# Attention scores: the product with the low parts of the keys on 128 rows, the low keys padded by rows of zeros

## The chip, the cores and the metric

The kernel runs on one core of a Trainium2 chip. The metric is the device time of one execution in microseconds (us); lower is better. The time before is the median of three runs.

## What is computed

The reference applies two layers to 1024 tokens of width 2048. A layer normalises the tokens, multiplies them by a wide input matrix, runs three mixers side by side (sliding-window attention, a gated spatial mixer, gated linear attention), gates their outputs, multiplies them by an output matrix and adds the result to the input. Only the scores of the attention matter here:

```python
scores = jnp.einsum('bnqgrd,bnkgd->bngrqk', qb, kb) * (SWA_HEAD_DIM ** -0.5)
```

There are 16 query heads of 64 dimensions in 4 groups; a group of 4 query heads shares one key head. The 1024 tokens are cut into blocks of 128 queries, and a block sees 256 keys: its own block and the one before it.

## The kernel before, in words

Each layer is worked in two halves of 512 tokens, so there are four phases, each an input part and an output part. Nearly all of TensorE's work is in the projections, `mm_f` (lines 390 to 392) and `mm_t` (lines 382 to 384). An fp32 value is split there into a high part in fp32r and a low part that holds the rest; a product is made of three matmuls (high by high, high by low, low by high). The weights come by DMA into `wraw`, ScalarE rounds them to their high part (line 368), VectorE subtracts to get the low part (line 369), and the pair stands in `whl`, of which there are three buffers.

The mixers run between these projections. They are generators in lanes (`att`, `gla`, `sg`, `mod`); `tick` is called after each k-tile of a projection's output tile and steps the lanes that are due. So the order in which the work is written down is fixed by counts of projection matmuls; the framework then orders each engine's instructions by priority when the program is built, and each engine runs its list in that order.

In an attention step, `att_split` has made `qs`, a tile with two heads p = 0 and 1. For each of them it holds the high part of the query on 64 of the 128 rows, and its low part on the other 64. `split_keys` has made, for each key head g, `kh[g]`, which holds the high part of the key on both halves of the rows, so that one matmul on 128 rows gives high by high plus low by high. The low parts of two key heads share one tile `kl[j]`: that of head 2j on rows 0 to 63, that of head 2j + 1 on rows 64 to 127. The third product, the query's high part by the key's low part, therefore runs on 64 rows. The scores of a block go into a PSUM tile `mx` that is shared by two blocks (b = 0, 1), one such tile for each p; PSUM has two `mx` buffers for all the mixers. The first block of the sequence has no block before it, so its matmuls take 128 columns and not 256. After the scores, ScalarE and VectorE copy them out of PSUM (lines 503 to 506).

In a phase there are 8 attention steps of 2 block pairs, each with 2 blocks and 2 heads, so 64 products with `kh` and 64 with `kl`. VectorE also carries the last 128 keys of the first half over to the second half (lines 459 and 463).

Of the kernel before, what the change touches and what calls it, by code (L numbers as in the profile page):

```python
# [10 lines left out]
F32 = mybir.dt.float32  # L11
F32R = mybir.dt.float32r
# [4 lines left out]
ALU = mybir.AluOpType  # L17
# [4 lines left out]
P = 128  # L22
# [4 lines left out]
H = SEQ // NH  # L27
# [13 lines left out]
def hybrid_kernel(ctx: ExitStack, tc: tile.TileContext, a, y_out):  # L41
# [11 lines left out]
    pools = {}  # L53

    V, S, G, PE = nc.vector, nc.scalar, nc.gpsimd, nc.tensor

    def load(out, in_):
        nc.sync.dma_start(out=out, in_=in_)
# [9 lines left out]
    def start(name, gen):  # L68
        lanes.setdefault(name, [deque(), None, 0])[0].append(gen)
# [36 lines left out]
    def mxt():  # L106
        return mx.tile([P, 512], F32, tag="mx", name="mx")
# [4 lines left out]
    def col(n, name):  # L112
        return sm.tile([P, n], F32, tag=name, name=name)
# [301 lines left out]
    def att():  # L415
        return pools["at"].tile([P, 512], F32, tag="at", name="at")

    def rope(dst, raw, cst):
        sh = att()
        V.stream_shuffle(sh, raw, swap)  # L420
        V.tensor_tensor(dst, raw, cst[0], ALU.mult)
        V.tensor_tensor(sh, sh, cst[1], ALU.mult)
        V.tensor_tensor(dst, dst, sh, ALU.add)
# [29 lines left out]
    def split_keys(j, kr, first):  # L453

        for p in range(2):
            g = 2 * j + p
            r, o = slice(64 * p, 64 * p + 64), slice(64 - 64 * p, 128 - 64 * p)
            if not first:
                V.tensor_copy(kh[g][:, 0:P], kh[g][:, H:H + P].bitcast(F32))
            S.copy(kh[g][r, P:], kr[r])  # L460
            S.copy(kh[g][o, P:], kr[r])
        if not first:
            V.tensor_copy(kl[j][:, 0:P], kl[j][:, H:H + P].bitcast(F32))
        for p in range(2):
            r = slice(64 * p, 64 * p + 64)
            V.tensor_tensor(kl[j][r, P:], kr[r], kh[2 * j + p][r, P:].bitcast(F32), ALU.subtract)

    def att_split(q):

        qs = pools["qs"].tile([P, 2, H], F32R, tag="qs", name="qs")  # L470
        for p in range(2):
            r, o = slice(64 * p, 64 * p + 64), slice(64 - 64 * p, 128 - 64 * p)
            S.copy(qs[r, p], q[r])
            V.tensor_tensor(qs[o, p], q[r], qs[r, p].bitcast(F32), ALU.subtract)
        return qs

    def attention(l, h, g0, qt, vt, cst):

        rope(qt[0], qt[0], cst)
        yield 5  # L480
        qs = att_split(qt[0])
        yield 6
        for m in range(4):
            i = 4 * g0 + m
            j = i // 4
            M = pools["m"].tile([P, 2, NT, P], F32, tag="M", name="M")
            for bp in range(2):
                sps = [mxt().rearrange("p (b k) -> p b k", b=2) for _ in range(2)]
                for b in range(2):
                    n = 2 * bp + b  # L490
                    k0 = P if h == 0 and n == 0 else 0
                    for p in range(2):
                        PE.matmul(sps[p][:, b, k0:], lhsT=qs[:, p, n * P:(n + 1) * P],  # L493
                                  rhs=kh[2 * j + p][:, n * P + k0:n * P + 256], start=True, stop=False)
                    for p in range(2):
                        rows = slice(64 * p, 64 * p + 64)
                        PE.matmul(sps[p][:, b, k0:], lhsT=qs[rows, p, n * P:(n + 1) * P],  # L497
                                  rhs=kl[j][rows, n * P + k0:n * P + 256], start=False, stop=True)
                for p in range(2):
                    sp = sps[p]  # L500
                    if h == 0 and bp == 0:
                        G.memset(M[:, p, 0], -1e30)
                        S.copy(M[:, p, 1], sp[:, 1, 0:P])
                    else:
                        S.copy(M[:, p, 2 * bp:2 * bp + 2], sp[:, :, 0:P])  # L505
                    V.copy_predicated(M[:, p, 2 * bp:2 * bp + 2], pmask.unsqueeze(1).broadcast_to([P, 2, P]),  # L506
                                      sp[:, :, P:2 * P])
                yield LAG["s"][bp]
            Mf = M.rearrange("p a b k -> p (a b) k")
            mxv = col(8, "at_mx")  # L510
            V.tensor_reduce(mxv, Mf, AX.X, ALU.max)
            nm = col(8, "at_nm")
            ns = nsink[l][:, 2 * i:2 * i + 2].unsqueeze(2).broadcast_to([P, 2, NT])
            V.scalar_tensor_tensor(nm.rearrange("p (a b) -> p a b", a=2), mxv.rearrange("p (a b) -> p a b", a=2),  # L514
                                   -0.125, ns, ALU.mult, ALU.min)
            es = col(8, "at_es")
            V.tensor_tensor(es.rearrange("p (a b) -> p a b", a=2), nm.rearrange("p (a b) -> p a b", a=2), ns,
                            ALU.subtract)
            S.activation(es, es, AF.Exp)
            den = col(8, "at_den")  # L520
            for k in range(8):
                S.activation(Mf[:, k], Mf[:, k], AF.Exp, bias=nm[:, k:k + 1], scale=0.125, accum_out=den[:, k:k + 1])  # L522
            V.tensor_tensor(den, den, es, ALU.add)
            V.reciprocal(den, den)
            V.tensor_tensor(Mf, Mf, den.unsqueeze(2).broadcast_to([P, 8, P]), ALU.mult)
            if m < 3:
                yield 4
                rope(qt[m + 1], qt[m + 1], cst)
                yield 5
                qs = att_split(qt[m + 1])  # L530
                yield LAG["e"] - 9
            else:
                yield LAG["e"]
            pts = []
            for p in range(2):
                tp = mxt()
                for n in range(NT):
                    PE.transpose(tp[:, n * P:(n + 1) * P], M[:, p, n], ident)  # L538
                pt = pools["pt"].tile([P, 2, NT, P], F32, tag="PT", name="PT")
                V.tensor_tensor(pt, tp.rearrange("p (n q) -> p n q", n=NT).unsqueeze(1).broadcast_to([P, 2, NT, P]),  # L540
                                amask.unsqueeze(2).broadcast_to([P, 2, NT, P]), ALU.mult)
                pts.append(pt)
                yield LAG["t"][p]
            yp = mxt()
            for n in range(NT):
                prev = not (h == 0 and n == 0)
                for w in range(2 if prev else 1):
                    for p in range(2):
                        g = 2 * j + p
                        vv = vt[n + 1 - w]  # L550
                        PE.matmul(yp[64 * p:64 * p + 64, n * P:(n + 1) * P], lhsT=vv[:, g * 64:g * 64 + 64],  # L551
                                  rhs=pts[p][:, w, n], start=(w == 0), stop=(w == 1 or not prev))
            yt = att()
            S.activation(yt, yp, AF.Copy, scale=0.5)
            load(y_d[h][i], yt)
            yield 2
# [198 lines left out]
    def in_phase(l, h, slots, pre=None):  # L755
# [18 lines left out]
        def keys(kraw):  # L774
            for j in range(2):
                rope(kraw[j], kraw[j], cst)
                yield 5
                split_keys(j, kraw[j], h == 0)
                yield 5
# [23 lines left out]

        qt = evac(4, io_tile, proj_f(512, slots))
        start("att", attention(l, h, 0, qt, vt, cst))
        cv = evac(4, hold, proj_t(512, slots))
        start("gla", gla_b(cv))
        ps = proj_f(512, slots)
        drain("att", until=lambda: lanes["att"][1] is None)
        qt = evac(4, io_tile, ps)  # L810
        start("att", attention(l, h, 1, qt, vt, cst))

        ps = proj_t(512, slots)
# [198 lines left out]
    with tc.tile_pool(name="start", bufs=1) as st:  # L1012
# [92 lines left out]
        for c in range(8):  # L1105
            for q in range(8):
                mod_load(8 * c + q + WM0 - 1)
                w = ws.popleft()
                for kk in range(2):
                    k = 2 * q + kk  # L1110
                    r = 32 * (k % 4)
# [40 lines left out]
                       ("ma", 1), ("kk", 1)):  # L1152
        pools[name] = ctx.enter_context(tc.tile_pool(name=name, bufs=bufs))
    kh = [pools["kk"].tile([P, P + H], F32R, name=f"kh{g}") for g in range(4)]
    kl = [pools["kk"].tile([P, P + H], F32R, name=f"kl{j}") for j in range(2)]
    start("mod", iter((60,)))
    for n in range(4):
        start("mod", mod_chunk(0, 8 + n))
# [115 lines left out]
```

## Time and profile before

| what | value |
|---|---|
| median of 3 runs | 3167.28 us (3166.84 to 3167.59) |
| the profiled execution | 3170.71 us, its span 3169.0 us |
| TensorE matmuls (PE) | 3095.0 us busy, 98% of the span, 17346 matmuls |
| TensorE weight loads (PEld) | 2459.1 us, 78% |
| VectorE (DVE) | 1838.1 us, 58% |
| ScalarE (ACT) | 1207.0 us, 38% |
| GpSimd (POOL) | 41.3 us, 1% |
| mean granted clock of TensorE | 0.990 of full speed |

The profiled execution took 3170.71 us, of which 3169.0 us lie between the first and the last instruction. A busy share says how long at least one instruction of the engine was in flight. Matmuls follow each other in a pipeline, so one is in flight longer than the distance from its start to the next one's start; it is this distance that a long row of matmuls costs.

### The profile page before, as it was taken

To read this page: it belongs to the slowest core of one execution; us is meant where nothing else is said; L and a number is where in the kernel's file an instruction comes from. 1 tells how busy PE (TensorE), PEld (TensorE's weight loads), DVE (VectorE), ACT (ScalarE), POOL (GpSimd) and SP (SyncE) were. 2 spreads that over 40 slices of the span, in tenths; PEclk is the share of its full clock that TensorE was granted. 3 is DMA by queue.
4 is the path that set the end of the run, shared out by engine and by line. 5 is a ranking of instruction groups with operands and counts; after the bars stand their busy time and mean duration, and the time that the engine had idled before them with its cause. 6 is when DMAs were issued, how large, how long until landed. Compare 5 with 4: busy or idle time off the path is not lost.

```text
span 3169.0 us, 44364 instructions
## 1 busy us (share of the span) xinstructions
PE 3095.0 (98%) x17346; PEld 2459.1 (78%) x17346; DVE 1838.1 (58%) x2953; ACT 1207.0 (38%) x2399; POOL 41.3 (1%) x80
## 2 busy tenths in 40 slices
PE   6999999999999999999999999999999999999998
PEld 2477777888878777888888877788888877788886
DVE  3268777665676877745355676644346475653425
ACT  3144437332344444323234454432223544432323
POOL 2000000000000000000000000000000000000000
PEclk8999999999999999999999999999999999999999
DMA  9754446566676335544346322334446322333535
GB/s 330 231 162 135 134 129 194 184 194 205 199 232 193 118 115 164 181 142 149 120 120 188 94 75 89 111 112 135 121 125 203 97 83 84 103 120 111 165 103 167
DMA packets 224195, 468.99 MB, mean 148 GB/s; under 512 B 21584, under 2 KB 77296, under 8 KB 223984
## 3 DMA queue, kind: packets, MB, share of 16 engines
q1 hardware_dynamic: 223984, 466.15, 47.8%
q8 instruction: 136, 2.23, 0.3%
q14 instruction: 75, 0.61, 0.1%
HBM read 429.37 MB, written 36.70 MB: 147 GB/s over the span
## 4 chain that ended last, share of the span: by engine, by line
PE 82%; DVE 7%; DMA 7%; ACT 2%; issue 2%; SPq 0%; DVEq 0%; ACTq 0%
PE pj L382 13%; PE pj L383 12%; PE pj L384 12%; PE pj L390 12%; PE pj L392 11%; PE pj L391 11%; DMA wm<-in_w_mod_dram 4%; PE mx L551 2%; PE mx L497 2%; PE mx L493 1%; PE pj L1112 1%; DVE ma L225 1%; DVE whl L369 1%; DMA t<-in_gla_norm_g_dram 1%; PE mx L538 1%
## 5 line engine op out<-in xcount | busy, mean ns | idle before, releaser
L369 DVE TENSOR_TENSOR whl<-wraw,whl 128x1024 fp32r<-128x1024 f32 (+3 forms) x512 | 590.9, 1154 | 740.7 <-ACT whl L368 739.0
L368 ACT CAST whl<-wraw 128x1024 fp32r<-128x1024 f32 (+3 forms) x512 | 509.0, 994 | 1108.3 <-PE pj L392 508.5
L390 PE MATMUL pj<-whl,act 128*128 128x512 f32 (+1 forms) x2048 | 792.2, 387 | 1.4 <-ACT whl L368 1.0
L392 PE MATMUL pj<-whl,act 128*128 128x512 f32 (+1 forms) x2048 | 779.7, 381 | 0.0
L391 PE MATMUL pj<-whl,act 128*128 128x512 f32 (+1 forms) x2048 | 777.5, 380 | 1.1 <-DVE whl L369 1.1
L382 PE MATMUL pj<-act,whl 128*128 128x512 f32 x1904 | 753.8, 398 | 3.6 <-ACT whl L368 1.9
L384 PE MATMUL pj<-act,whl 128*128 128x512 f32 x1904 | 745.6, 392 | 1.3 <-DVE whl L369 1.2
L383 PE MATMUL pj<-act,whl 128*128 128x512 f32 x1904 | 744.8, 391 | 0.3 <-DVE act L279 0.3
L390 PEld LDWEIGHTS pj<-whl,act 128*128 128x128 f32 x2048 | 386.1, 189 | 79.6 <-issue 6.0
L392 PEld LDWEIGHTS pj<-whl,act 128*128 128x128 f32 x2048 | 386.1, 189 | 73.9 <-issue 0.7
L391 PEld LDWEIGHTS pj<-whl,act 128*128 128x128 f32 x2048 | 386.6, 189 | 69.7 <-DVE whl L369 1.7
L382 PEld LDWEIGHTS pj<-act,whl 128*128 128x128 f32 x1904 | 357.5, 188 | 103.9 <-issue 20.4
L384 PEld LDWEIGHTS pj<-act,whl 128*128 128x128 f32 x1904 | 358.0, 188 | 85.5 <-issue 7.3
L383 PEld LDWEIGHTS pj<-act,whl 128*128 128x128 f32 x1904 | 358.4, 188 | 77.4 <-issue 5.9
L225 DVE SCALAR_TENSOR_TENSOR ma<-wm,sc,ma 128x512 f32<-128x512 f32 x240 | 179.8, 749 | 107.6 <-DMA wm<-in_w_mod_dram 105.2
L522 ACT ACTIVATE M<-M,at_nm 128x128 f32<-128x128 f32 x256 | 99.4, 390 | 47.6 <-DVE at_nm L514 45.1
L506 DVE COPY_PREDICATED M<-pmask,mx 128x256 f32<-128x256 uint8 x128 | 51.6, 443 | 91.4 <-ACT M L505 79.0
L540 DVE TENSOR_TENSOR PT<-mx,amask 128x1024 f32<-128x1024 f32 x64 | 78.0, 1220 | 24.3 <-PE mx L538 24.2
L1112 PE MATMUL pj<-wm,scb 128*32 128x512 f32 x256 | 66.8, 666 | 24.5 <-DMA wm<-in_w_mod_dram 24.5
L505 ACT COPY M<-mx 128x256 f32<-128x256 f32 x96 | 32.0, 375 | 133.0 <-PE mx L497 132.9
L551 PE MATMUL mx<-PT,v 128*64 128x128 f32 x960 | 67.9, 287 | 12.1 <-DVE PT L540 12.1
L551 PEld LDWEIGHTS mx<-PT,v 128*64 128x64 f32 x960 | 57.2, 143 | 26.7 <-DVE PT L540 14.8
(229 smaller groups left out, 2391.4 us busy)
## 6 DMA issues: line engine op xcount, KB each, us to landing
wraw<-in_w_in_dram SPq DMA_DIRECT2D x312, 512.0 KB, 3.6
wraw<-in_w_out_dram SPq DMA_DIRECT2D x136, 512.0 KB, 3.6
wm<-in_w_mod_dram SPq DMA_DIRECT2D x256, 256.0 KB, 3.3
wm<-in_w_mod_dram SPq DMA_DIRECT2D x64, 512.0 KB, 6.2
y<-at SPq DMA_DIRECT2D x64, 256.0 KB, 2.6
q<-y SPq DMA_DIRECT2D x64, 256.0 KB, 3.3
q<-x SPq DMA_DIRECT2D x36, 256.0 KB, 2.8
wraw<-in_w_vcg_dram SPq DMA_DIRECT2D x32, 272.0 KB, 2.8
```

The costliest lines, as they stand in the source:

```text
L225: V.scalar_tensor_tensor(acc, ws[k], sc[:, k:k + 1], acc, ALU.mult, ALU.add)
L368: S.copy(hl[:, 0], raw)
L369: V.tensor_tensor(hl[:, 1], raw, hl[:, 0].bitcast(F32), ALU.subtract)
L382: PE.matmul(ps, lhsT=whi, rhs=slot[:, 0], start=(k == 0), stop=False)
L383: PE.matmul(ps, lhsT=whi, rhs=slot[:, 1], start=False, stop=False)
L384: PE.matmul(ps, lhsT=wlo, rhs=slot[:, 0], start=False, stop=(k == NK - 1))
L390: PE.matmul(ps, lhsT=slot[:, 0, c], rhs=whi, start=(k == 0), stop=False)
L391: PE.matmul(ps, lhsT=slot[:, 0, c], rhs=wlo, start=False, stop=False)
L392: PE.matmul(ps, lhsT=slot[:, 1, c], rhs=whi, start=False, stop=(k == NK - 1))
L522: S.activation(Mf[:, k], Mf[:, k], AF.Exp, bias=nm[:, k:k + 1], scale=0.125, accum_out=den[:, k:k + 1])
L551: PE.matmul(yp[64 * p:64 * p + 64, n * P:(n + 1) * P], lhsT=vv[:, g * 64:g * 64 + 64], rhs=pts[p][:, w, n], start=(w == 0), stop=(w == 1 o ...
L1112: PE.matmul(mps[r:r + 32, :], lhsT=scb[:, k], rhs=w[:, kk], start=(k < 4), stop=(k >= 12))
```

## The change

The low keys get a tile for each key head, `kl[0]` to `kl[3]`, of 128 rows. The head's low keys stand on the same 64 rows as before; the other 64 rows are set to zero once, at the start, by GpSimd. The third product of the scores then takes all 128 rows of `qs` and of `kl`: the query's low part, which is on the other 64 rows, meets zeros. The order in the source also changes, from both heads' `kh` products followed by both heads' `kl` products, to `kh` and `kl` of one head followed by those of the other. In `split_keys` the copy of the last 128 keys is made for each head on 64 rows, and not for both heads together on 128 rows.

```diff
             S.copy(kh[g][r, P:], kr[r])
             S.copy(kh[g][o, P:], kr[r])
-        if not first:
-            V.tensor_copy(kl[j][:, 0:P], kl[j][:, H:H + P].bitcast(F32))
-        for p in range(2):
-            r = slice(64 * p, 64 * p + 64)
-            V.tensor_tensor(kl[j][r, P:], kr[r], kh[2 * j + p][r, P:].bitcast(F32), ALU.subtract)
+            if not first:
+                V.tensor_copy(kl[g][r, 0:P], kl[g][r, H:H + P].bitcast(F32))
+            V.tensor_tensor(kl[g][r, P:], kr[r], kh[g][r, P:].bitcast(F32), ALU.subtract)
...
                     for p in range(2):
-                        PE.matmul(sps[p][:, b, k0:], lhsT=qs[:, p, n * P:(n + 1) * P],
-                                  rhs=kh[2 * j + p][:, n * P + k0:n * P + 256], start=True, stop=False)
-                    for p in range(2):
-                        rows = slice(64 * p, 64 * p + 64)
-                        PE.matmul(sps[p][:, b, k0:], lhsT=qs[rows, p, n * P:(n + 1) * P],
-                                  rhs=kl[j][rows, n * P + k0:n * P + 256], start=False, stop=True)
+                        for part, keys in enumerate((kh, kl)):
+                            PE.matmul(sps[p][:, b, k0:], lhsT=qs[:, p, n * P:(n + 1) * P],
+                                      rhs=keys[2 * j + p][:, n * P + k0:n * P + 256], start=(part == 0), stop=(part == 1))
...
-    kl = [pools["kk"].tile([P, P + H], F32R, name=f"kl{j}") for j in range(2)]
+
+    kl = [pools["kk"].tile([P, P + H], F32R, name=f"kl{g}") for g in range(4)]
+    for g in range(4):
+        G.memset(kl[g][64 - 64 * (g % 2):P - 64 * (g % 2)].bitcast(F32), 0.0)
```

## Rows read from the trace of the kernel before

**Rows 1.** The page's busy time: share of the span and count by engine.

```profile
PE 3095.0 (98%) x17346; PEld 2459.1 (78%) x17346; DVE 1838.1 (58%) x2953; ACT 1207.0 (38%) x2399; POOL 41.3 (1%) x80
```

**Rows 2.** The page's chain that ended last, by engine.

```profile
PE 82%; DVE 7%; DMA 7%; ACT 2%; issue 2%; SPq 0%; DVEq 0%; ACTq 0%
```

**Rows 3.** Engines' busy us (count), sum of 270:512, 1048:1290, 1790:2040, 2540:2790, each with attention.

```profile
sum 984.00, PE 964.34 PEld 756.09 DVE 678.07 ACT 431.45 POOL 4.95; mean PE 241.09 PEld 189.02 DVE 169.52 ACT 107.86 POOL 1.24
```

**Rows 4.** Waits of ScalarE and of TensorE: us in total, times, longest.

```profile
ACT whl L368 <- PE pj L392: 508.5, 156, 6.2
...
PE mx L551 <- DVE PT L540: 12.1, 5, 4.2
```

**Rows 5.** Groups of score matmuls by line: durations in ns, minimum, median, maximum.

```profile
L493 PE MATMUL mx<-kh,qs x256: 218/282/580, 271.8 to 2784.8; 128*128 128x256 f32 x105, 128*128 128x128 f32 x23
...
L497 PE MATMUL mx<-kl,qs x256: 322/381/579, 272.1 to 2785.0; 64*128 64x256 f32 x106, 64*128 64x128 f32 x22
```

**Rows 6.** Timeline of TensorE, both heads together: start, us, engine, line, operation.

```profile
2783.94 0.40 PE L493 MATMUL mx<-kh,qs 128*128 128x256 f32 x2
2784.27 0.38 PE L497 MATMUL mx<-kl,qs 64*128 64x256 f32 x2
2784.58 0.50 PE L493 MATMUL mx<-kh,qs 128*128 128x256 f32 x2
2785.01 0.39 PE L497 MATMUL mx<-kl,qs 64*128 64x256 f32 x2
2785.33 0.50 PE L390 MATMUL pj<-whl,act 128*128 128x512 f32 x1
2785.67 0.40 PE L391 MATMUL pj<-whl,act 128*128 128x512 f32 x1
2785.90 0.39 PE L392 MATMUL pj<-whl,act 128*128 128x512 f32 x1
```

**Rows 7.** Timeline of TensorE, one head alone.

```profile
1052.12 0.28 PE L493 MATMUL mx<-kh,qs 128*128 128x256 f32 x1
1052.33 0.38 PE L497 MATMUL mx<-kl,qs 64*128 64x256 f32 x1
1052.63 0.38 PE L493 MATMUL mx<-kh,qs 128*128 128x256 f32 x1
1052.95 0.38 PE L497 MATMUL mx<-kl,qs 64*128 64x256 f32 x1
1053.26 0.50 PE L392 MATMUL pj<-whl,act 128*128 128x512 f32 x1
1053.60 0.40 PE L390 MATMUL pj<-whl,act 128*128 128x512 f32 x1
```

**Rows 8.** Timeline of TensorE: first `kl` product alone, first pair, last one alone.

```profile
272.06 0.32 PE L497 MATMUL mx<-kl,qs 64*128 64x128 f32 x1
...
277.23 0.53 PE L497 MATMUL mx<-kl,qs 64*128 64x256 f32 x2
...
2754.75 0.38 PE L497 MATMUL mx<-kl,qs 64*128 64x256 f32 x1
```

**Rows 9.** Timeline of TensorE, a row of matmuls of 272 columns: first and twelfth.

```profile
205.15 0.29 PE L391 MATMUL pj<-whl,act 128*128 128x272 f32 x1
...
206.53 0.29 PE L390 MATMUL pj<-whl,act 128*128 128x272 f32 x1
```

**Rows 10.** Timeline of the weight loads, at the stretch of rows 9 and of rows 6.

```profile
205.15 0.19 PEld L392 LDWEIGHTS pj<-whl,act 128*128 128x128 f32 x1
...
2785.33 0.19 PEld L390 LDWEIGHTS pj<-whl,act 128*128 128x128 f32 x1
```

**Rows 11.** VectorE's copy and subtraction for `kl`, and a memset of GpSimd.

```profile
L466 DVE TENSOR_TENSOR kl<-t,kh x16: 676/686/692, 180.6 to 2464.1; 64x512 fp32r<-64x512 f32 x16
L463 DVE CAST kl<-kl x4: 210/217/223, 185.0 to 1717.7; 128x128 fp32r<-128x128 f32 x4
...
L601 POOL MEMSET hold<- 128x512 f32 x16 | 8.4, 527 | 1351.6 <-DMA x<-hold 647.1 <-DMA out_dram<-hold 329.8 <-DVE el L684 191.5
```

## The prediction

> **What bounds the kernel now.** I read four views in this order: the page's busy times, the chain of waits that ended last, the waits engine by engine, and then the timeline of TensorE where the change acts. The busy times show matmuls in flight for 98% of the span while VectorE has 58% and ScalarE 38% [rows 1]. That alone would not prove a bound, since a matmul in flight may be a waiting one. The chain shows the same from the other end: 82% of the span is TensorE's own work, VectorE and DMA come in with 7% each [rows 2]. The waits settle it. ScalarE, which starts the split of the weights, has waited 508.5 us for line 392 alone, that is, for a projection to give a weight buffer back, while TensorE's waits for the attention's transposed probabilities come to 12.1 us in the whole run [rows 4]. The helpers wait for TensorE and not the other way round. So a microsecond that TensorE saves in these stretches should come off the time nearly whole, as long as the others keep up.
>
> How much of TensorE's time can the scores be? The two lines have 256 matmuls each [rows 5]. Their durations don't tell, since matmuls overlap; the starts do. In the long row of 272-column matmuls on 128 rows, eleven steps take 206.53 − 205.15 = 1.38 us, 0.125 us each [rows 9], and a 512-column matmul is followed by the next after 2785.90 − 2785.67 = 0.23 us [rows 6]. The line through the two points gives about 0.12 us for 256 columns. Eight score products of a block pair would take 0.96 us at that pace. The timeline shows 1.50 us: from the first `kh` at 2783.94 to the second projection matmul after the scores at 2785.67 it is 1.73 us, of which 0.23 us belong to the first projection matmul [rows 6]. I count up to that second matmul because the first one, in flight for 0.50 us and followed after 0.34 us rather than 0.23, carries a part of the delay.
>
> Where the time goes can be read in the same lines. The two `kl` products, on rows 0 to 63 and 64 to 127, run side by side: both together are in flight for 0.39 us [rows 6], which is what one takes, 381 ns [rows 5]. But the next 128-row matmul starts only 0.31 to 0.32 us after them. The weight load shows why: in the steady row a load of 0.19 us begins while the matmul before is running, at 205.15 for the matmul that comes one step later; after a 64-row product the load begins at 2785.33, together with its own matmul [rows 10]. Each passage from 128 rows to 64 and back thus empties TensorE's pipeline.
>
> The passages don't always serve two heads. In other block pairs only one head's PSUM buffer was free when the order was made, and TensorE goes `kh`, `kl`, `kh`, `kl` for that head, some projection matmuls, and the same for the other head. Four products then take 1053.60 − 1052.12 − 0.23 = 1.25 us [rows 7], against 0.48 at the steady pace. Walking the timeline through all four phases I count 91 visits to 64 rows by a pair of `kl` products and 74 by one alone (2 × 91 + 74 = 256); the first and the last of each kind: pairs 277.23 [rows 8] to 2785.01 [rows 6], alone 272.06 to 2754.75 [rows 8].
>
> **The change part by part.** *The products.* After the change all 512 are 128-row matmuls like their neighbours, at 0.12 us.
> - A pair visit saves (1.50 − 0.96) / 2 = 0.27 us; 91 of them 24.6 us. The loss of the side-by-side run is in this figure: three product times become four.
> - A visit alone saves (1.25 − 0.48) / 2 = 0.385 us; 74 of them 28.5 us.
> - Together 53 us.
>
> The 64 products of 128 columns (32 on each line; the first block of the sequence) are in this as if they were 256 wide. By the line through the two paces they could take 0.06 us, which would add at most 64 × 0.06 = 4 us to the gain; the bounds of this term are 53 and 57.
>
> At this place a rule of the skill speaks for the change and another against it. The page TensorEngine Tiling (Array Packing) of the Trainium skill, Tiling Modes, says that changing the tiling mode drains TensorE; the delays behind the `kl` products agree with it, and by it the sum stands as above. The page TensorE: Matmul & The Clock Gate of the Trainium skill, Why this matters for your kernels, advises the opposite: a product of few rows takes as long as one of 128, and the gain of row slices is that several run at the same time, so this change would only lose. The pairs do run at the same time here, but by that rule alone the time would rise by 11 us; it is the first rival below.
>
> *The order of the source.* `kl` now follows `kh` of the same head, into the same PSUM columns. The 272-column row does just that, three products in turn into one tile, at 0.125 us [rows 9], so I give it no cost. If the order on TensorE still goes by heads when only one buffer is free, it costs nothing either, since there is no passage left.
>
> *VectorE and ScalarE.* The 16 subtractions stay as they are, 64 rows of 512. The 4 copies of 128 rows become 8 of 64; a copy took 217 ns [rows 11], and if 64 rows take as long, VectorE does 4 × 0.22 = 0.9 us more in the whole run. It is hidden: the subtractions begin at 180.6 [rows 11] and the first product that reads them at 272.1 [rows 5], 91 us later. Without that cover it would be those 0.9 us. The new order of the lines in `split_keys` may move a subtraction by one ScalarE copy; the same 91 us cover it.
>
> *GpSimd.* Four memsets of 64 rows by 640 columns. The nearest row has 512 columns on 128 rows at 527 ns [rows 11], so some 0.66 us each, 2.6 us on an engine that is busy for 1% [rows 1]. They come before the first subtraction and once only. At worst VectorE stands for these 2.6 us near 180 us with weight splits queued behind it; I count nothing, and keep 2.6 us for the range.
>
> *What comes late next.* In the four stretches with attention matmuls are in flight for 964.34 of 984.00 us, so 19.7 us are idle, and VectorE is busy for 678.07 us, 69% [rows 3]. Without 53 us the stretches last 931 us and VectorE's share is 73%. The stretches' idle time is bounded below by growing not at all; above, I let it double, 20 us. VectorE's load rises only by a twentieth, and the split's waits say that the buffers come from TensorE [rows 4], so I take a value near the lower end, 4 us.
>
> *Sum.* 53 − 4 = 49 us off the profiled execution's 3170.71 us gives 3121.7. That execution lies 3.4 us above the median of the three runs, 3167.28; against the median the same sum gives **3118 us**. Of the profiled time 1.7 us lie outside the span of 3169.0 and are untouched.
>
> **The rivals.**
> 1. *The delay does not come from the number of rows* (slower). It might come with short matmuls whose weights are new, or with the return to a PSUM tile just written, and stay. Then only the side-by-side run is lost: 91 × 0.12 = 11 us more, 3178 us. The price of the delay now is 0.39 us for a pair visit (0.27 + 0.12) and 0.385 for one alone, 64 us in all, so slower is decided when less than a sixth of it (11 of 64) goes. For it: two things change at each passage, the line and the rows. Against it: the 272-column matmuls are almost as short, have new weights each, write the same tile three times in a row and show no delay [rows 9]. Chance 0.04.
> 2. *Weight loads become the limit.* A load takes 0.19 us [rows 10]. If in the short products it could not run under the matmul before, a product would cost at least 0.19 rather than 0.12: 512 × 0.07 = 36 us of the 53 gone, 3150 us with no further loss. Against it stand the loads of 0.19 us that begin every 0.125 us [rows 9, 10]. Chance 0.04.
> 3. *The gain is had on TensorE and partly given back*: VectorE, a DMA or another order of the instructions around the scores takes half of it, 27 us; 3140 us. For it: VectorE has 69% in these stretches [rows 3], and attention steps are placed by counts of projection matmuls, which now go by faster. Against it: ScalarE's long waits for buffers [rows 4]. Chance 0.13.
> 4. *All of it is given back*, because the stretches are in truth set by a chain through VectorE: 3167 us. The idle time of only 19.7 us in 984 [rows 3] leaves little room. Chance 0.03.
>
> **How the numbers follow.** My forecast as told has the remaining chance, 0.76, and by itself a range of 3110 (57 us gained and no new wait, against the median) to 3130 (the 53 us less 13 us of waits and the memsets' 3). I let the range reach 4 us further down, for the paces that I read to 0.01 us (0.01 us on 512 products is 5 us), so it goes from 3106 to 3142, which takes in rival 3 as well; rivals 1, 2 and 4, 0.11 together, lie outside. A measurement of this kernel can tell about 0.2%, 6 us, from no change. Faster: the forecast, rival 2 and rival 3, 0.93, less 0.01 for the far end of rival 2 (at 0.22 us for a product the whole gain would be gone, 512 × 0.10 = 51 us): 0.92. Same: rival 4 and that 0.01: 0.04. Slower: rival 1, 0.04.
>
> **What would show it.** In the profile after, the score lines should have only 128-row forms; a block pair's eight products should take about 0.96 us from the first start to the second projection matmul, less 0.23, where it is 1.50 now; the weight load behind the last of them should begin before its own matmul. TensorE's idle time in the attention stretches should grow by no more than some microseconds, and each of the four stretches be shorter by about a quarter of the whole gain. The parts without attention should last as long as before. The prediction is wrong if starts 0.2 us or more apart remain between the score products (rivals 1 and 2), or if they are gone and the gaps stand elsewhere, at the probabilities' transposes or the weight splits (rivals 3 and 4).

## The result and the profile after

The changed kernel takes 0.9853 of the time before (95% interval 0.9839 to 0.9868), 1.5% less, or 46.6 us of 3167.44. Its four runs have a median of 3126.42 us (3122.08 to 3129.4). The two medians are 41.0 us apart, a little less than the interval gives (41.8 to 51.0 us), so the gain is known to within some 5 us. The profiled execution took 3122.08 us, 48.6 us less than the one profiled before; it was the fastest of its four. The forecast was 3118 us in a range of 3106 to 3142.

The page of the kernel after, its busy times and its chain by engine, answers to [rows 1, 2]:

```profile
span 3120.4 us, 44382 instructions
...
PE 3042.7 (98%) x17346; PEld 2448.0 (78%) x17346; DVE 1837.3 (59%) x2957; ACT 1206.2 (39%) x2399; POOL 43.4 (1%) x84
...
PE 82%; DVE 8%; DMA 5%; ACT 2%; issue 2%; SPq 0%; DVEq 0%; ACTq 0%
```

The count of matmuls is the same, 17346, and TensorE is still what bounds the kernel: 98% of the span and 82% of the chain. VectorE has four instructions more (the copies by head), GpSimd four (the memsets).

The timeline of TensorE after the change, for the block pair that stands in [rows 6]:

```profile
2735.33 0.40 PE L392 MATMUL pj<-whl,act 128*128 128x512 f32 x1
2735.56 0.28 PE L492 MATMUL mx<-kh,qs 128*128 128x256 f32 x1
2735.68 0.28 PE L492 MATMUL mx<-kl,qs 128*128 128x256 f32 x1
2735.80 0.28 PE L492 MATMUL mx<-kh,qs 128*128 128x256 f32 x1
2735.92 0.28 PE L492 MATMUL mx<-kl,qs 128*128 128x256 f32 x1
2736.04 0.28 PE L492 MATMUL mx<-kh,qs 128*128 128x256 f32 x1
2736.16 0.28 PE L492 MATMUL mx<-kl,qs 128*128 128x256 f32 x1
2736.28 0.28 PE L492 MATMUL mx<-kh,qs 128*128 128x256 f32 x1
2736.40 0.28 PE L492 MATMUL mx<-kl,qs 128*128 128x256 f32 x1
2736.52 0.39 PE L390 MATMUL pj<-whl,act 128*128 128x512 f32 x1
2736.75 0.40 PE L391 MATMUL pj<-whl,act 128*128 128x512 f32 x1
```

Every product starts 0.12 us after the one before it, and the projection matmul behind them is followed after 0.23 us as anywhere else. From the first start to the second projection matmul it is 1.19 us; less 0.23 that leaves 0.96, where [rows 6] gave 1.50. The weight loads of the same stretch answer to [rows 10]:

```profile
2736.28 0.19 PEld L492 LDWEIGHTS mx<-kl,qs 128*128 128x128 f32 x1
2736.40 0.19 PEld L390 LDWEIGHTS pj<-whl,act 128*128 128x128 f32 x1
2736.52 0.19 PEld L391 LDWEIGHTS pj<-whl,act 128*128 128x128 f32 x1
```

The load for L390's matmul, which starts at 2736.52, begins at 2736.40, together with the last `kl` product. Before, a load behind a `kl` product began with its own matmul.

Where did the 48.6 us come from? The windows below are cut in each kernel from its first to its last score product in a phase. First come the four windows of the kernel before and their sum, then those of the kernel after (columns: window; us; busy us and count of PE, PEld, DVE, ACT and POOL; granted clock of TensorE; busy share of the DMA engines; GB/s):

```profile
271.80:508.10 236.30, 227.13 (x1491) 176.64 (x1491) 173.22 (x296) 101.57 (x281) 2.47 (x14) 0.97 0.46 141
1050.40:1282.30 231.90, 227.77 (x1536) 177.88 (x1535) 171.17 (x292) 100.70 (x265) 0.00 (x0) 0.98 0.44 137
1812.30:2032.80 220.50, 218.06 (x1487) 171.40 (x1487) 141.36 (x246) 98.65 (x265) 2.48 (x14) 1.00 0.30 90
2560.90:2784.80 223.90, 221.66 (x1523) 174.45 (x1523) 140.12 (x242) 100.51 (x265) 0.00 (x0) 0.99 0.30 89
sum 912.60, PE 894.63 PEld 700.38 DVE 625.88 ACT 401.43 POOL 4.95; mean PE 223.66 PEld 175.09 DVE 156.47 ACT 100.36 POOL 1.24
```

```profile
270.50:493.80 223.30, 213.32 (x1492) 172.81 (x1493) 172.72 (x296) 101.14 (x281) 2.46 (x14) 0.98 0.48 148
1033.60:1253.10 219.50, 212.76 (x1535) 174.17 (x1536) 170.27 (x292) 100.35 (x265) 0.00 (x0) 0.99 0.47 144
1782.70:1995.10 212.40, 208.35 (x1489) 170.20 (x1488) 141.22 (x246) 98.65 (x265) 2.48 (x14) 0.99 0.31 93
2522.80:2736.30 213.50, 210.08 (x1525) 172.50 (x1525) 139.87 (x242) 100.09 (x265) 0.00 (x0) 0.99 0.31 92
sum 868.70, PE 844.51 PEld 689.68 DVE 624.09 ACT 400.22 POOL 4.94; mean PE 211.13 PEld 172.42 DVE 156.02 ACT 100.06 POOL 1.24
```

The four stretches are 43.9 us shorter. Matmuls are in flight for 50.1 us less, and TensorE's idle time in them grew from 18.0 to 24.2 us (912.60 − 894.63, 868.70 − 844.51), 6.2 us. VectorE does the same work as before, in less time: its share went from 69% to 72%. The granted clock of the four stretches was 0.97, 0.98, 1.00 and 0.99 before and 0.98, 0.99, 0.99 and 0.99 after; by an estimate from these figures (length times the missing share) some 3 us of the 43.9 go with the clock and not with the products, and why it differs is not shown. The other 4.7 us lie outside these stretches. TensorE is idle there for 2.9 us less than before, all of it ahead of the second stretch; executions of one kernel differ by more (fifteen of the kernel before lie between 3166.36 and 3176.27 us), so this is not shown to be the change's doing.

### The profile page after: what moved, and what is told of

Read it like the earlier page. It is cut to its first block, busy times and chain, and to the rows that moved or that the text cites. A ratio compares the mean times of both kernels' runs of the same rounds, so it can differ in the third digit from the quotient of the medians.

```text
span 3120.4 us, 44382 instructions
## 1 busy us (share of the span) xinstructions
PE 3042.7 (98%) x17346; PEld 2448.0 (78%) x17346; DVE 1837.3 (59%) x2957; ACT 1206.2 (39%) x2399; POOL 43.4 (1%) x84
## 4 chain that ended last, share of the span: by engine, by line
PE 82%; DVE 8%; DMA 5%; ACT 2%; issue 2%; SPq 0%; DVEq 0%; ACTq 0%
PE pj L382 13%; PE pj L383 12%; PE pj L384 12%; PE pj L390 12%; PE pj L392 12%; PE pj L391 12%; DMA wm<-in_w_mod_dram 2%; PE mx L546 2%; PE mx L492 2%; PE pj L1107 1%; DVE whl L369 1%; DMA t<-in_gla_norm_g_dram 1%; DVE ma L225 1%; DMA t<-in_x_dram 1%; PE mx L533 1%
## 5 line engine op out<-in xcount | busy, mean ns | idle before, releaser
L390 PE MATMUL pj<-whl,act 128*128 128x512 f32 (+1 forms) x2048 | 785.5, 384 | 1.0 <-ACT whl L368 1.0
L390 PEld LDWEIGHTS pj<-whl,act 128*128 128x128 f32 x2048 | 385.3, 188 | 72.7 <-issue 5.6
L1107 PE MATMUL pj<-wm,scb 128*32 128x512 f32 x256 | 67.0, 665 | 24.2 <-DMA wm<-in_w_mod_dram 24.2
L501 DVE COPY_PREDICATED M<-pmask,mx 128x256 f32<-128x256 uint8 x128 | 51.6, 442 | 57.3 <-ACT M L500 48.5
```

Of the source, the lines that this page charges most:

```text
L390: PE.matmul(ps, lhsT=slot[:, 0, c], rhs=whi, start=(k == 0), stop=False)
L1107: PE.matmul(mps[r:r + 32, :], lhsT=scb[:, k], rhs=w[:, kk], start=(k < 4), stop=(k >= 12))
```

## The experiments

Three theories were put to the test. **V**: each visit of TensorE to 64 rows costs about 0.39 us beyond its products, the change takes all 165 visits away, and that is the whole gain, less 0.12 us for each pair that no longer runs side by side. **O**: the gain comes from the new order, `kl` right behind `kh` of the same head, with the same weights and the same PSUM tile. **S**: it comes from the separate `kl` tiles and the waits that go with them.

**e1, the padded rows in the old order.** The edit is shown against the kernel after.

```diff
-                    for p in range(2):
-                        for part, keys in enumerate((kh, kl)):
+                    for part, keys in enumerate((kh, kl)):
+                        for p in range(2):
                             PE.matmul(sps[p][:, b, k0:], lhsT=qs[:, p, n * P:(n + 1) * P],
```

> The low keys padded by zeros and all products on 128 rows, but in the order of the source before: both heads' kh, then both heads' kl. Theory V (each visit of TensorE to 64 rows costs about 0.39 us; the change takes all 165 visits away): as the changed kernel, 3126 us, within 10 us; a block pair's eight products 0.96 us. Theory O (the gain comes from the order, kl right behind kh of the same head, with the same weights and the same PSUM tile): most of the gain is lost, 3155 to 3178 us.

Measured: 0.9859 of the time before (0.9846 to 0.9873), median 3125.79 us. Each of the two ratios, this one and the changed kernel's 0.9853, lies in the other's interval. With 128 rows the order is worth nothing that can be measured, which speaks against O.

**e2, the new order on 64 rows.** The edit is shown against the kernel before.

```diff
                     for p in range(2):
                         PE.matmul(sps[p][:, b, k0:], lhsT=qs[:, p, n * P:(n + 1) * P],
                                   rhs=kh[2 * j + p][:, n * P + k0:n * P + 256], start=True, stop=False)
-                    for p in range(2):
                         rows = slice(64 * p, 64 * p + 64)
                         PE.matmul(sps[p][:, b, k0:], lhsT=qs[rows, p, n * P:(n + 1) * P],
```

> kl stays on 64 rows in the two shared tiles; only the order of the source is that of the change, kh and kl of one head, then of the other. In the program's order TensorE goes to 64 rows 254 times, where the kernel before does 165 times. Theory V: 89 visits more at 0.39 us, and about 89 fewer side-by-side runs at 0.12 us: 35 + 11 = 46 us slower than before, 3213 us. Theory O: as the changed kernel, about 3126 us.

Measured: 1.0136 (1.0122 to 1.015), which is 43 us more than before, where V gave 46. The median is 3213.11 us; that it meets V's 3213 to the microsecond is chance, since the kernel before had a median of 3171.14 us beside it. The timeline of one block pair in this kernel:

```profile
2829.84 0.28 PE L493 MATMUL mx<-kh,qs 128*128 128x256 f32 x1
2830.05 0.38 PE L496 MATMUL mx<-kl,qs 64*128 64x256 f32 x1
2830.36 0.38 PE L493 MATMUL mx<-kh,qs 128*128 128x256 f32 x1
2830.67 0.38 PE L496 MATMUL mx<-kl,qs 64*128 64x256 f32 x1
2830.98 0.38 PE L493 MATMUL mx<-kh,qs 128*128 128x256 f32 x1
2831.30 0.38 PE L496 MATMUL mx<-kl,qs 64*128 64x256 f32 x1
2831.61 0.38 PE L493 MATMUL mx<-kh,qs 128*128 128x256 f32 x1
2831.92 0.38 PE L496 MATMUL mx<-kl,qs 64*128 64x256 f32 x1
2832.23 0.50 PE L390 MATMUL pj<-whl,act 128*128 128x512 f32 x1
2832.57 0.40 PE L391 MATMUL pj<-whl,act 128*128 128x512 f32 x1
```

Four visits instead of two: 2832.57 − 2829.84 − 0.23 = 2.50 us, and (2.50 − 0.96) / 4 = 0.385 us for each visit, the price that [rows 7] gave. The order is that of the change line for line, and the weights come from the same `qs`; what differs from the timeline of the kernel after is the rows (and the shared `kl` tile, which e4 shows to cost nothing). O is refuted.

**e3, 64 rows, but half as many visits.** The second block of a pair does `kl` before `kh`, so that the `kl` products of both blocks follow each other. The edit is against the kernel before; the lines that it takes out are left out here.

```diff
...
+                    for part in ("hi", "lo") if b == 0 else ("lo", "hi"):
+                        first = (part == "hi") == (b == 0)
                         for p in range(2):
...
+                            PE.matmul(sps[p][:, b, k0:], lhsT=qs[rows, p, n * P:(n + 1) * P],
+                                      rhs=keys[rows, n * P + k0:n * P + 256], start=first, stop=not first)
```

> kl stays on 64 rows in the two shared tiles; in the second block of a pair kl goes ahead of kh, so that the kl products of both blocks follow each other. In the program's order TensorE goes to 64 rows 87 times (before: 165). Theory V: 78 visits fewer at 0.39 us: 30 us faster than before, 3137 us. If the delay belonged to each kl product or to the change of tile and not to the visit, it would stay at 3167 us.

Measured: 0.9913 (0.9898 to 0.9928), median 3144.78 us, 27 to 28 us less than before by the ratio, where V gave 30. The same products on the same rows cost less when they are visited together:

```profile
410.15 0.40 PE L392 MATMUL pj<-whl,act 128*128 128x512 f32 x1
410.39 0.40 PE L499 MATMUL mx<-kh,qs 128*128 128x256 f32 x2
410.71 0.50 PE L499 MATMUL mx<-kl,qs 64*128 64x256 f32 x4
411.15 0.51 PE L499 MATMUL mx<-kh,qs 128*128 128x256 f32 x2
411.49 0.40 PE L390 MATMUL pj<-whl,act 128*128 128x512 f32 x1
411.73 0.40 PE L391 MATMUL pj<-whl,act 128*128 128x512 f32 x1
```

One visit: 411.73 − 410.39 − 0.23 = 1.11 us. Four `kh` at 0.12, two pairs side by side at 0.12 and one visit at 0.39 make 0.48 + 0.24 + 0.39 = 1.11.

**e4, all of the change but its products.** The products are those of before, on 64 rows; each reads its head's own tile. The line shown is the one in which the products differ from those of the kernel before.

```diff
-                                  rhs=kl[j][rows, n * P + k0:n * P + 256], start=False, stop=True)
+                                  rhs=kl[2 * j + p][rows, n * P + k0:n * P + 256], start=False, stop=True)
```

> All of the change but its products: four kl tiles with zero rows, the memsets, the copies by head; the products read 64 rows in the old order. 165 visits as before. Theory V: as before, 3167 us, within 6 us. Theory S (the separate tiles, and waits of VectorE that go with them, bring the gain): about 3126 us.

Measured: 1.0005 (0.9997 to 1.0014). The tiles, memsets and copies cost and bring nothing that can be told from no change. S is refuted.

**e5, no zeros.** The rows that the change pads hold the low keys too. The edit is against the kernel after.

```diff
-                V.tensor_copy(kl[g][r, 0:P], kl[g][r, H:H + P].bitcast(F32))
+                V.tensor_copy(kl[g][:, 0:P], kl[g][:, H:H + P].bitcast(F32))
             V.tensor_tensor(kl[g][r, P:], kr[r], kh[g][r, P:].bitcast(F32), ALU.subtract)
+            V.tensor_tensor(kl[g][o, P:], kr[r], kh[g][r, P:].bitcast(F32), ALU.subtract)
...
-    for g in range(4):
-        G.memset(kl[g][64 - 64 * (g % 2):P - 64 * (g % 2)].bitcast(F32), 0.0)
```

> The changed kernel without the zeros and the memsets: the other 64 rows of each kl tile hold the low keys as well, so the low query by low key product is added (a fourth term that the other kernels leave out), at the price of 16 more subtractions on VectorE, 0.69 us each, 11 us in all. Theory V: the matmuls don't care what stands in the rows; as the changed kernel, 3126 us, within 6 us. If the zeros themselves helped (a higher granted clock, or less work), it would be slower than that, towards 3167 us, at a lower clock.

Measured: 0.9868 (0.9851 to 0.9884), median 3129.85 us, granted clock 0.992 against 0.991. The interval holds the changed kernel's 0.9853. What stands in the other rows makes no difference that can be told, and the 16 subtractions more are hidden.

**e6 and e7, the length of a visit.** Both make each `kl` product five times, e6 on 64 rows in the order of e3, e7 on 128 rows in the order of the change. This is the main line of e7's edit, against the kernel after; e6 makes the same repetition in e3's loop.

```diff
-                        for part, keys in enumerate((kh, kl)):
+                        for part, keys in enumerate((kh, kl, kl, kl, kl, kl)):
...
```

> The kernel with fewer visits, each kl product made five times on 64 rows (the low part of the scores is five times too large; its time alone counts): 1024 products more, about as many visits (85). Theory V with the two heads side by side for most of them: some 870 at 0.06 us and the rest at 0.12 us: 70 us more than the kernel with fewer visits, about 3215 us. Without a gain from running side by side: 1024 x 0.12 = 123 us more, 3268 us.

> The changed kernel with each kl product made five times on 128 rows (the low part of the scores five times too large, as in the run beside it): 1024 products more at 0.12 us, 123 us: 3249 us. Theory V: here the kernel on 64 rows should be the faster of the two, since a visit costs 0.39 us and a pair side by side saves 0.12 us, so that a visit pays from about three and a quarter pairs on. If 128 rows are better whatever the length of a visit, this one stays 20 us or more below the other.

Measured: e6 1.0212 (1.0196 to 1.0229), median 3238.8 us; e7 1.0269 (1.0254 to 1.0284), 3257.92 us. With long visits the 64 rows win by 0.57% of the time before, 18 us, where the forecasts were 34 apart. By the ratios e7 takes 132 us more than the changed kernel, where 123 were forecast (0.129 us for each of the 1024 products), and e6 95 us more than e3, where 70 were forecast. A long visit in e6:

```profile
392.30 1.45 PE L498 MATMUL mx<-kl,qs 64*128 64x256 f32 x18
393.68 0.50 PE L498 MATMUL mx<-kh,qs 128*128 128x256 f32 x2
```

Its 18 products take 1.38 us to the next `kh`, 0.077 each with the way out included, so side by side they take well under 0.12 each. Adding up the starts as above, e6's score stretches take 159.9 us against 87.1 in e3, 73 us more, as forecast. Most of the rest is idle time of TensorE up to its last matmul, 82.3 us against 63.1. Of these 19.2 us, 12.0 are waits for VectorE's copy of the scores out of PSUM: 14.0 us in e6 (6.4, 4.5 and 3.1 for L498, L658 and L715) against 2.0 in e3. In e7 the score stretches take 191.4 us. So on TensorE the 64 rows win by 31.5 us, near the 34 of the forecasts; of that the profiled executions keep 22 us (3257.09 − 3235.04), since e6 has 4 us more idle time than e7 (82.3 against 78.2) and a lower granted clock (0.990 against 0.992, some 6 us by an estimate from the two spans).

**All together.** Adding up, in each trace, the time from the first score product of a stretch to the second projection matmul behind it, less 0.227 us (the step of a 512-column matmul), gives what the scores cost TensorE:

| kernel | visits to 64 rows | score time, us | ratio of times |
|---|---|---|---|
| after | 0 | 65.0 | 0.9853 |
| e1 | 0 | 65.7 | 0.9859 |
| e3 | 87 | 87.1 | 0.9913 |
| before | 165 | 115.1 | 1 |
| e4 | 165 | 114.6 | 1.0005 |
| e2 | 254 | 159.0 | 1.0136 |

From e3 to before it is 28.0 us for 78 visits, 0.36 each. From before to e2 it is 43.9 us, of which 89 pairs that no longer run side by side take 10.7, so 33.2 us for 89 visits, 0.37 each. The sums take in what little of the scores ran while the clock was low, so the price is known to some hundredths of a microsecond. None of the experiments is faster than the changed kernel by more than the noise (e1, with the same products, is level with it).

## Why the prediction was right

**The bound.** That time saved on TensorE comes off nearly whole held: 50.1 us less of score time, 48.6 us off the profiled execution. The 48.6 are the 50.1 less 6.2 of new idle time in the attention stretches, plus 4.7 from the parts outside them.

**The price of a visit.** 0.27 us for a pair and 0.385 for a single one were read from one place each; the sum of 53 us was 3 too high. The side before was right: 512 products at 0.12 us and 53 us of delay make 114.4 us, and 115.1 were measured. The side after was not: the products run at 0.12 us each in the undisturbed row, but over all 512 it is 65.0 / 512 = 0.127 us. In the trace after, 70 products are followed only after more than 0.13 us, 4.5 us beyond 0.12 in all, which covers the difference. [rows 6] also show where a visit's price lies: about 0.09 us on the way in (two `kh` products take 0.33 us to the first `kl`, for 0.24 at the steady pace), 0.19 until the next 128-row matmul starts (0.31 for 0.12), and 0.11 on that matmul (0.34 for 0.23).

The upper bound of 57 us, for 128-column products that take half as long, did not come true. The line through the paces of 272 and 512 columns does not reach down to 128. One of the places where the first block of the sequence is worked after the change, products and then weight loads:

```profile
296.78 0.22 PE L492 MATMUL mx<-kh,qs 128*128 128x128 f32 x1
296.83 0.28 PE L492 MATMUL mx<-kl,qs 128*128 128x128 f32 x1
296.95 0.27 PE L492 MATMUL mx<-kh,qs 128*128 128x128 f32 x1
297.06 0.27 PE L492 MATMUL mx<-kl,qs 128*128 128x128 f32 x1
297.17 0.33 PE L492 MATMUL mx<-kh,qs 128*128 128x256 f32 x1
...
296.78 0.19 PEld L492 LDWEIGHTS mx<-kl,qs 128*128 128x128 f32 x1
296.89 0.19 PEld L492 LDWEIGHTS mx<-kh,qs 128*128 128x128 f32 x1
297.00 0.19 PEld L492 LDWEIGHTS mx<-kl,qs 128*128 128x128 f32 x1
```

Only the first product, behind a 512-column matmul, is followed after 0.05 us; the others start 0.11 us apart (the median of all 64 is 0.11), and the weight loads begin 0.11 us apart too, each some 0.06 us ahead of its own product (the load at 296.78 is that of the product at 296.83). So at 128 columns the pace goes with the loads and not with the columns, and 0.12 us for 256 columns lies just above it. No run changes the loads alone, so that they set the pace is the reading that fits, and not shown.

**The two rules.** That a pair runs side by side is true here (e6), and that a passage to other rows costs time of its own is true too (e2, e3). On the page TensorEngine Tiling (Array Packing) of the Trainium skill, Tiling Modes, changing the tiling mode drains TensorE, and these runs agree, at 0.36 to 0.39 us a visit. The advice of TensorE: Matmul & The Clock Gate of the Trainium skill, Why this matters for your kernels, to give products of few rows their own row slices, pays here only for visits that are long enough: with visits of at most two pairs e3 is slower than the changed kernel, with visits of mostly ten pairs e6 is faster than e7.

**VectorE, GpSimd.** The groups of VectorE's copies and GpSimd's memsets in the kernel after:

```profile
L463 DVE CAST kl<-kl 64x128 fp32r<-64x128 f32 x8 | 1.8, 219 | 0.2
...
L1153 POOL MEMSET kl<- 64x640 f32 x4 | 2.5, 629 | 112.9 <-PE pj L384 112.7
```

The copies took 219 ns on 64 rows as on 128, and 0.9 us more in all; the memsets 2.5 us, where 2.6 were expected. Neither shows in the time (e4).

**What came late next.** Idle time in the attention stretches grew by 6.2 us, where I took 4 of at most 20. (The top of my own range counted 13 of waits where this bound would give 20; nothing hung on it.) The longest of TensorE's waits after the change, apart from those for the weights `wm` at the start:

```profile
PE mx L546 <- DVE PT L535: 13.9, 4, 4.4
```

That is the wait for the transposed probabilities, 12.1 us before [rows 4]. TensorE's waits for VectorE's copy of the scores (L501, 4.7 us) are new in part: 1.1 us before. The parts without attention, which I expected to last as long as before, gave 4.7 us, of which 2.9 are less idle time; the rest is not settled.

**The rivals.** The first, a delay that does not come from the rows, is refuted by e2 and the kernel after together: in the same order the delays are there on 64 rows and gone on 128. The second, loads as the limit, did not happen at 256 columns, where products with loads of 0.19 us start every 0.12 us; but at 128 columns the products do keep the pace of the loads, at 0.11 us and not at 0.19, and the 4 us that the bound of 57 would have added did not come. The third, half of the gain given back, did not come true: it was 6 us of 50 at most. The fourth did not happen.

**The size.** Against its own profile the sum was 49 us and 48.6 were measured. That close a match is in part luck: 3 us too much from the products and 2 too little for the waits are made good by 4.7 us outside the attention stretches that were not in the forecast. The median of the runs after is 8 us above the forecast of 3118; those runs spread over 7 us, by the ratio the gain is 46.6 us, and e1 and e5, with the same 512 products on 128 rows, give 45 and 42 us by theirs. The mechanism, the visits and their price, was right; the gain itself is some 2 to 8 us smaller than the 49 of the forecast.

## What to carry to other kernels

Look at the starts, not at the durations: a short run of matmuls on another number of rows costs its passage, here 0.36 to 0.39 us for each visit, and that stands in the weight load that begins only with its own matmul. Half-row products side by side save 0.12 us a pair, so by an estimate from these two figures a visit pays from about 0.39 / 0.12, three and a quarter pairs of this size, on. Measured are only the two sides, visits of at most two pairs and of mostly ten. For shorter visits fill the rows up, with zeros or with anything that adds nothing, or put the visits together. Count the visits in the order in which the engine runs them, not in the source: here one source loop became 91 visits of two and 74 of one.

## What the runs showed of the hardware that was not expected

A 128-column product on 128 rows starts 0.11 us after the one before it, hardly less than the 0.12 us of 256 columns, where the weight loads begin 0.11 us apart too. A copy of 64 rows by 128 columns took as long on VectorE (219 ns) as one of 128 rows (217 ns [rows 11]), so packing two heads into one tile had saved four copies, 0.9 us of VectorE's time, and nothing that the run times show (e4). And the fourth term of the scores, the low query by the low key, costs nothing measurable in e5, whose matmuls are the same 512 on 128 rows.
